# Alternating expert places, a blocked gather, a down product on four column quarters and a sum into x on four row tiles

## The chip, the cores and the metric

The kernel runs on one core of one Trainium2 chip. The metric is device time in microseconds (us). The kernel before takes 1996.44 us, the median of three runs (1993.87 to 1998.35).

The names of the profile: PE is TensorE, PEld its weight loads, DVE VectorE, ACT ScalarE, POOL GpSimd. SP is the engine that issues all transfers here (SPq is its queue). L1545 is line 1545 of the kernel before.

## The reference

Two layers on 256 latent tokens and 256 context tokens of width 1024, all in float32. The even layer has attention beside a convolution and then a dense feed-forward block; the odd layer has a state-space mixer and then the expert block. This is the part that the change touches:

```python
def moe_swiglu(h, w_router, w1, w3, w2):
    ...
    logits = (hf @ w_router).astype(jnp.float32)
    top_v, top_i = lax.top_k(logits, TOP_K)
    top_w = jax.nn.softmax(top_v, axis=-1)
    gates = jnp.sum(jax.nn.one_hot(top_i, N_EXPERTS, dtype=jnp.float32) * top_w[..., None], axis=1)
    out = jnp.zeros_like(hf)
    for e in range(N_EXPERTS):
        out = out + gates[:, e:e + 1].astype(hf.dtype) * swiglu(hf, w1[e], w3[e], w2[e])
```

with `swiglu = (silu(h @ w1) * (h @ w3)) @ w2`, 8 experts, 2 for each token, a hidden width of 3584. Only the 256 latent tokens go through it. The weights of the eight experts are 8 x 3 x 1024 x 3584 x 4 bytes = 352 MB. After the sum into x comes a last RMSNorm.

## The kernel before

The kernel computes the two layers one after the other; the change leaves all work up to the router as it is. In the expert stage each expert's tokens are gathered into slots of 32, called groups. There are eight **places**, worked off in order. Place 0 is always expert 0; the other seven experts are ranked by their token counts (`places`, L1579) and put in places 1 to 7 from the fullest on. The number of groups of each place is fixed in the program (`G`, L1429): 3, 3, 3, 3, 2, 2, 2, 2. Behind the last place two further passes over all places stand under a condition, for tokens that did not fit (`moe`, L1643).

The work of a place is a list of units (`expert`, L1471). `gather` (L1432) selects the tokens by a product with a 0/1 matrix `pm` and scales them, result `xe`. `up` multiplies by w1, then w3: first the hidden rows 0 to 2047, then 2048 to 3583. The weights are the moving operand and 32 tokens of `xe` the stationary one, so that four column tiles of TensorE work beside one another, each on another part of the weights (L1491: 512 columns each in the first part, 384 in the second). `turn` transposes the hidden activations to `hT` (L1514). `down` (L1545) multiplies them by w2, 512 columns at a time: two halves of the 1024 outputs, and for each half two partial sums on the four column tiles, result `y`, one PSUM bank for each group. `scatter` multiplies `y` by the layer's gate row `g2` (L1555), and brings it back to token order by a product with the transposed map `PT` (L1562; two row tiles of 64, which also add the two partial sums), and DVE adds it with the gate of the router into x (L1566). `PT` comes from transposes of `pm` on TensorE (L1466) with a copy by ACT.

Each place reads 46 weight **transfers** (`load`, L131): 16 of 1 MiB for the first part of w1 and w3 (8 KB in a row per partition), 16 of 768 KB for the second part (6 KB rows), 14 of 1 MiB for w2 (two rows of 4 KB). They go through a **ring** of 16 buffers of 1 MiB, in the fixed order of use; `run` (L150) issues up to `AHEAD` = 14 transfers ahead of the unit that it writes out. A transfer waits on SP until the matmuls that read its buffer last are done. All transfers are issued by SP in one order; the expert's number for places 1 to 7 is read into SP's registers first (L1606). PSUM has five banks under the name `h` and three under `y` (L1779).

The gather of the next place and the map's transposes are spread between the units (`later`); the scatter of a place comes two units into the next place. A scheduler then settles each engine's order; the instructions of an engine run in that order.

Of the kernel before, what the change touches and what calls it, by code (L numbers as in the profile page):

```python
# [19 lines left out]
P = 128  # L20
D = 1024
# [6 lines left out]
NCONST = 1032  # L28


def host_consts():

    kc = np.zeros((P, NCONST), np.float32)
# [18 lines left out]
    for j in range(4):  # L52
        kc[32 * j:32 * j + 8, C_SEL8:C_SEL8 + 8] = np.eye(8)
    return kc


class Pair:
# [4 lines left out]
    def __call__(self, k, s=slice(0, 512)):  # L62
        return tuple(t[k // 4][:, k % 4, s] for t in self.t)

# [11 lines left out]
class Net:  # L76
# [44 lines left out]
    def load(self, view, pool=None):  # L121

        pieces = view if isinstance(view, list) else [(slice(0, P), view)]
# [161 lines left out]
    def columns2(self):  # L285
        A, cols, row = self.A, self.cols_fn, self.row_fn
        kc = self.ecp.tile([P, NCONST - C_LE], F32, name="kc")
        self.nc.sync.dma_start(kc, A["kc"][:, C_LE:])
# [1084 lines left out]
    def route(self):  # L1373
# [4 lines left out]
        self.h2 = mp.tile([P, 2, D], F32, name="h2")  # L1378
        m8 = rt.tile([P, 2, 8], F32, name="m8")
# [41 lines left out]
        self.g2 = mp.tile([P, 512], F32, name="g2r")  # L1421
        g2 = self.g2row.rearrange("k p -> (k p)")
        for i in range(2):
            nc.sync.dma_start(self.g2[64 * i:64 * i + 64], g2[512 * i:512 * i + 512].partition_broadcast(64))
# [4 lines left out]
    G = [3, 3, 3, 3, 2, 2, 2, 2]  # L1429
    SS = ((0, 512), (2048, 384))  # L1430

    def gather(self, e, pos, n_g):  # L1432
# [4 lines left out]
        Pm = self.wk([P, 2, 3, 4, 32], "pm", bufs=2)[:, :, :n_g]  # L1437
        x = self.wk([P, KD, 96], "xe", bufs=2)[:, :, :n]
        PT = self.wk([P, 3, 256], "PT", bufs=2)

        def work():
            slots = self.iota[:, :n].rearrange("p (g t) -> p g t", g=n_g).unsqueeze(2).to_broadcast([P, n_g, 4, 32])
            for b in range(2):
                nc.vector.tensor_scalar(Pm[:, b], slots, pos[:, b, e:e + 1], None, op0=ALU.is_equal)
            yield
            for q in range(2):
                pt = self.ps("h")
                for i in range(4):
                    k = 4 * q + i
                    for b in range(2):  # L1450
                        nc.tensor.matmul(pt[:, i * n:(i + 1) * n].rearrange("p (g t) -> p g t", g=n_g),  # L1451
                                         self.h2[:, b, k * P:(k + 1) * P], Pm[:, b, :, 0], start=b == 0, stop=b == 1)
# [7 lines left out]
                yield  # L1460

        def turn():
            for g in range(n_g):
                pt = self.ps("h")
                for b in range(2):
                    nc.tensor.transpose(pt[:, b * P:(b + 1) * P], Pm[:, b, g].rearrange("p r t -> p (r t)"), self.ident)  # L1466
                nc.scalar.copy(PT[:, g], pt[:, 0:256])
# [332 lines left out]
```

## Time and profile before

| | |
|---|---|
| median of 3 runs | 1996.44 us (1993.87 to 1998.35) |
| profiled execution | 1998.1 us |
| its span, first to last instruction | 1996.3 us, granted TensorE clock 0.975 of 2.4 GHz |
| PE busy | 1860.1 us (93%) |
| DVE, ACT, POOL busy | 734.5, 519.0, 257.7 us |
| HBM read | 485.14 MB, 244 GB/s over the span |
| expert stage, place 0 to the end | 1088.7 to 1996.3 us |

How to read the profile: a busy share says how long an engine had an instruction in it, not that it did its best. The chain of waits starts at the last instruction and goes back, at each step to what released it; an engine or a transfer that stands on it in a stretch sets the time of that stretch. In the view by time, the idle time before a row and its releaser stand in brackets. Matmuls in float32 take two passes, so the profile counts two instructions where the program has one.

### The profile page before, as it was taken

Reading aid. Unit: us, or ns where it says so; the run is one execution under the profiler, and the core shown is the slowest. Engines: PE = TensorE matmul, PEld = TensorE weight load, DVE = VectorE, ACT = ScalarE, POOL = GpSimd, SP = SyncE. Lnnn points to the kernel's source line nnn. Section 1 sums busy time; section 2 is a strip of 40 time slices with the busy share of each in tenths; the row PEclk is TensorE's granted clock in tenths of the full one; section 3 lists DMA queues with packets and bytes.
Section 4 is the critical chain, followed back from the end, with each engine's and each line's share of the span. In section 5 each row is a group of like instructions: output and inputs, shape, how many; then the busy total and the mean of one; then the engine's idle time right before and its main releaser. Section 6 shows DMA issues by size and latency. Waiting matters only on the chain.

```text
span 1996.3 us, 29959 instructions
## 1 busy us (share of the span) xinstructions
PE 1860.1 (93%) x12586; PEld 1057.2 (53%) x12586; DVE 734.5 (37%) x1079; ACT 519.0 (26%) x948; POOL 257.7 (13%) x239
## 2 busy tenths in 40 slices
PE   6999999999999989899898999999999999979795
PEld 3685366888888868666566343433434343313121
DVE  3496545333343458988975000101001011101011
ACT  3434443222223247466653000000000000000000
POOL 0154000000000024476650000000000000000000
PEclk8999989999999999999898999999999999999998
DMA  8544575323322332221338999898998999999996
GB/s 295 179 136 155 202 201 179 127 85 106 106 85 95 117 118 85 84 64 64 116 127 313 306 418 364 336 403 289 416 344 342 415 389 416 413 417 413 418 413 236
DMA packets 136429, 488.31 MB, mean 245 GB/s; under 512 B 10432, under 2 KB 15192, under 8 KB 119896
## 3 DMA queue, kind: packets, MB, share of 16 engines
q1 hardware_dynamic: 136280, 486.25, 65.0%
q8 instruction: 103, 1.69, 0.4%
q14 instruction: 46, 0.38, 0.1%
HBM read 485.14 MB, written 1.07 MB: 244 GB/s over the span
## 4 chain that ended last, share of the span: by engine, by line
PE 69%; DMA 14%; DVE 10%; ACT 2%; issue 2%; POOL 1%; SPq 0%; DVEq 0%; ACTq 0%; POOLq 0%
PE h L1491 20%; PE g L226 9%; PE g L227 9%; PE g L228 9%; DMA t<-in_od_ex_w_dram 9%; PE y L1545 8%; DVE cv L1055 5%; DMA raw<-in_od_ex_w_dram 4%; PE h L1562 2%; PE g L330 1%; PE h L1451 1%; PE o L758 1%; PE g L735 1%; DVE whl L147 1%; DMA raw<-in_ev_w_in_dram 1%
## 5 line engine op out<-in xcount | busy, mean ns | idle before, releaser
L1491 PE MATMUL h<-t,xe 128*32 128x384 f32 (+1 forms) x2880 | 288.4, 541 | 13.5 <-DMA t<-in_od_ex_w_dram 13.3
L227 PE MATMUL g<-t,whl 128*128 128x512 f32 (+1 forms) x608 | 237.7, 391 | 0.0
L228 PE MATMUL g<-t,whl 128*128 128x512 f32 (+1 forms) x608 | 236.1, 394 | 0.7 <-POOL whl L147 0.7
L226 PE MATMUL g<-t,whl 128*128 128x512 f32 (+1 forms) x608 | 233.3, 395 | 1.4 <-ACT opad L1033 0.7
L1491 PE MATMUL h<-raw,xe 128*32 128x512 f32 (+1 forms) x2240 | 223.3, 540 | 8.1 <-DMA raw<-in_od_ex_w_dram 8.1
L147 DVE TENSOR_TENSOR whl<-raw,whl 128x1024 fp32r<-128x1024 f32 x109 | 138.6, 1274 | 201.0 <-ACT whl L144 200.6
L144 ACT CAST whl<-raw 128x1024 fp32r<-128x1024 f32 x129 | 134.7, 1050 | 265.6 <-PE g L228 231.2
L1491 PEld LDWEIGHTS h<-t,xe 128*32 128x32 f32 x2880 | 92.0, 110 | 195.3 <-issue 167.9
L1502 DVE TENSOR_TENSOR g<-g,h 128x512 f32<-128x512 f32 (+1 forms) x40 | 24.8, 621 | 458.3 <-PE h L1491 365.4
L411 POOL TENSOR_SCALAR rsv<-sst 128x1 f32<-128x1 f32 (+1 forms) x15 | 5.5, 364 | 1353.6 <-DVE sst L404 1353.5
L227 PE MATMUL g<-whl,t 128*128 128x512 f32 (+1 forms) x432 | 169.3, 394 | 6.4 <-DVE whl L147 3.2
L228 PE MATMUL g<-whl,t 128*128 128x512 f32 (+1 forms) x432 | 166.8, 394 | 0.0
L226 PE MATMUL g<-whl,t 128*128 128x512 f32 (+1 forms) x432 | 162.4, 395 | 2.9 <-DVE t L624 1.4
L1491 PEld LDWEIGHTS h<-raw,xe 128*32 128x32 f32 x2240 | 73.7, 110 | 150.9 <-issue 134.7
L1545 PE MATMUL y<-t,hT 128*32 128x512 f32 x1288 | 144.9, 594 | 8.7 <-DMA t<-in_od_ex_w_dram 8.6
L226 PEld LDWEIGHTS g<-t,whl 128*128 128x128 f32 x608 | 116.0, 192 | 30.1 <-issue 2.3
L228 PEld LDWEIGHTS g<-t,whl 128*128 128x128 f32 x608 | 116.0, 191 | 25.3 <-issue 1.9
L227 PEld LDWEIGHTS g<-t,whl 128*128 128x128 f32 x608 | 116.4, 191 | 23.4 <-issue 0.9
L1519 ACT COPY hT<-h 128x512 f32<-128x512 f32 (+1 forms) x24 | 12.8, 533 | 418.1 <-PE h L1514 417.8
L1545 PE MATMUL y<-raw,hT 128*32 128x512 f32 x952 | 107.9, 594 | 8.8 <-DMA raw<-in_od_ex_w_dram 8.8
L1545 PEld LDWEIGHTS y<-t,hT 128*32 128x32 f32 x1288 | 43.0, 110 | 103.0 <-issue 77.8
L227 PEld LDWEIGHTS g<-whl,t 128*128 128x128 f32 x432 | 82.5, 191 | 27.0 <-DVE whl L147 4.7
(348 smaller groups left out, 2189.3 us busy)
## 6 DMA issues: line engine op xcount, KB each, us to landing
t<-in_od_ex_w_dram SPq DMA_DIRECT2D x135, 1024.0 KB, 12.9
raw<-in_od_ex_w_dram SPq DMA_DIRECT2D x105, 1024.0 KB, 13.9
t<-in_od_ex_w_dram SPq DMA_DIRECT2D x72, 768.0 KB, 9.3
raw<-in_od_ex_w_dram SPq DMA_DIRECT2D x56, 768.0 KB, 10.8
raw<-in_ev_ff_w_dram SPq DMA_DIRECT2D x32, 1024.0 KB, 5.2
raw<-in_ev_ada_w_dram SPq DMA_DIRECT2D x24, 1024.0 KB, 6.9
raw<-in_od_ada_w_dram SPq DMA_DIRECT2D x24, 1024.0 KB, 5.3
raw<-in_od_w_in_dram SPq DMA_DIRECT2D x20, 1024.0 KB, 5.2
```

The lines of the kernel that those rows point to most:

```text
L144: self.nc.scalar.copy(hv, v[:, k0:k0 + m])
L147: eng.tensor_tensor(lv, v[:, k0:k0 + m], hv.bitcast(F32), op=ALU.subtract)
L226: mm(out, l[0], r[0], start=start, stop=False)
L227: mm(out, l[0], r[1], start=False, stop=False)
L228: mm(out, l[1], r[0], start=False, stop=stop)
L330: nc.tensor.matmul(st["p"][32 * j:32 * j + 32], self.cs[:, k, 6 - 2 * i:38 - 2 * i], wv, start=k < 4, stop=k >= 4, tile_position=(0, 32 * j))
L735: nc.tensor.matmul(sc[c][:, :nk], self.qT[s, r, b * P:(b + 1) * P], self.kT[s, :nk], start=True, stop=True, tile_position=(64 * c, 0))
L1055: nc.vector.scalar_tensor_tensor(v, pads[i + j][:, 0:ns, t:t + 256], self.cvw(t, c0 + i + j), v, op0=ALU.mult, op1=ALU.add)
L1491: nc.tensor.matmul(st[i][g][32 * p:32 * p + 32, :n], st["x"][:, k, 32 * g:32 * g + 32], wv[:, n * p:n * p + n], start=k == 0, stop=k == KD ...
L1502: nc.vector.tensor_mul(st["g"][g], st["g"][g], st[1][g][:, :n])
L1545: nc.tensor.matmul(st["y"][g][r:r + 32], st["hT", s][:, c, g, 32 * p:32 * p + 32], w[:, 512 * half:512 * half + 512], start=s == 0 and k == 1,
L1562: nc.tensor.matmul(pt[half], st["PT"][r, g, b * P:(b + 1) * P], ys[r, g], start=g == 0, stop=g == n_g - 1, tile_position=(64 * half, 0))
```

## The change

Only the expert stage changes.

- The places have 3, 2, 3, 2, 3, 2, 3, 1 groups, and the ranks are put in them in the order 3, 0, 4, 1, 5, 2, 6 (0 is the fullest of the seven).
- `gather` builds `pm` once, without the four copies, and runs as one unit between the second `up` and the second `turn` of the place before.
- `PT` is no longer transposed on TensorE. The positions of all tokens are transposed once, written to DRAM (`posd`), and for each place read back by a transfer that spreads its row to all partitions (`prow`, 128 KB in 512-byte runs); DVE compares it with the slot numbers.
- `down` works on four quarters of 256 columns, one for each column tile; each column tile holds the whole sum of its quarter, two groups share a bank. `y` is multiplied by `g2` right behind it. Twelve of a place's 14 w2 transfers now take pairs of consecutive rows, 8 KB in one piece; the hidden activations are transposed in the matching order.
- The sum into x takes four row tiles of 32, each with its quarter of 256 columns, in four banks of `h`; DVE adds eight pieces of 256 columns. It is one unit behind the first `up` of the next place.
- The ring has 17 buffers, 16 transfers go ahead, PSUM has six banks `h` and two `y`. The expert's number is read when a place's first transfer is written out.

```diff
+C_SLOT, C_RANK, C_CAP = NCONST, NCONST + 3, NCONST + 10
...
+GROUPS = (3, 2, 3, 2, 3, 2, 3, 1)
+RANKS = (3, 0, 4, 1, 5, 2, 6)
...
+    kc[:, C_SLOT:C_SLOT + 3] = i[:, None] % 32 + 32 * np.arange(3)
+    kc[:, C_RANK:C_RANK + 7] = RANKS
+    kc[:, C_CAP:C_CAP + 8] = 32 * np.array(GROUPS)
...
-        self.g2 = mp.tile([P, 512], F32, name="g2r")
+        self.g2 = mp.tile([P, 256], F32, name="g2r")
...
-    G = [3, 3, 3, 3, 2, 2, 2, 2]
     SS = ((0, 512), (2048, 384))
 
-    def gather(self, e, pos, n_g):
+    def gather(self, e, n_g):
...
-        Pm = self.wk([P, 2, 3, 4, 32], "pm", bufs=2)[:, :, :n_g]
+        Pm = self.wk([P, 2, 96], "pm", bufs=2)[:, :, :n]
         x = self.wk([P, KD, 96], "xe", bufs=2)[:, :, :n]
...
-        def turn():
-            for g in range(n_g):
-                pt = self.ps("h")
-                for b in range(2):
-                    nc.tensor.transpose(pt[:, b * P:(b + 1) * P], Pm[:, b, g].rearrange("p r t -> p (r t)"), self.ident)
-                nc.scalar.copy(PT[:, g], pt[:, 0:256])
-                yield
-        return x, PT, work(), turn()
...
+    def slot_map(self, e, n_g):
+
+        nc = self.nc
+        r = self.wk([P, 256], "prow", bufs=2)
+        nc.sync.dma_start(r.rearrange("p (b t) -> p b t", b=2), self.posd[:, e].partition_broadcast(P))
+        PT = self.wk([P, 3, 256], "PT", bufs=2)
+        for g in range(n_g):
+            nc.vector.tensor_scalar(PT[:, g], r, self.slot[:, g:g + 1], None, op0=ALU.is_equal)
+        return PT
+
+    def pos_rows(self, pos):
+
+        nc = self.nc
+        self.pos = pos
+        pt = self.ps()
+        nc.tensor.transpose(pt[:16, 0:P], pos.rearrange("p b e -> p (b e)"), self.ident)
+        r = self.wk([16, P], "posr", bufs=1)
+        nc.scalar.copy(r, pt[:16, 0:P])
+        d = self.drp.tile([16, P], F32, name=self.nm("posd"))
+        nc.sync.dma_start(d, r)
+        self.posd = d.rearrange("(b e) p -> b e p", b=2)
...
         def down(s):
-            nch = self.SS[s][1] // P
+            r0, n = 4 * self.SS[s][0] // 4, self.SS[s][1]
+            rows = lambda r, m: (lambda w: w[:, r:r + m])
+            pair = lambda w: w.rearrange("o (i j) n -> i (o j) n", j=2)
+
+            pieces = []
+            for p in range(4):
+                for c in range(n // 256):
+                    f = rows(r0 + n * p + 256 * c, 256)
+                    pieces.append((lambda w, f=f: pair(f(w)), [(p, 2 * c), (p, 2 * c + 1)]))
+            if n % 256:
+                for p in (0, 2):
+                    f = rows(r0 + n * p, 2 * n)
+                    pieces.append((lambda w, f=f: f(w).rearrange("o (s i) n -> i (o s) n", s=2)[n - P:n],
+                                   [(p, n // P - 1), (p + 1, n // P - 1)]))
 
             def begin():
                 if s == 0:
-                    st["y"] = [self.ps("y") for _ in range(n_g)]
+                    st["y"] = [self.ps("y") for _ in range(0, n_g, 2)]
 
             def mm(k, wv, _):
-
-                p, c = divmod(k, nch)
-                st["w", k % 2] = wv, p, c
-                if k % 2 == 0:
-                    return
+                p, c = pieces[k // 2][1][k % 2]
                 for g in range(n_g):
-                    for half in range(2):
-                        for j in range(2):
-                            w, p, c = st["w", j]
-                            r = 64 * half + 32 * j
-                            nc.tensor.matmul(st["y"][g][r:r + 32], st["hT", s][:, c, g, 32 * p:32 * p + 32],
-                                             w[:, 512 * half:512 * half + 512], start=s == 0 and k == 1,
-                                             stop=s == 1 and k == 4 * nch - 1, tile_position=(0, r))
-
-            k0 = 16 * s
-            return Unit([w2[:, k0 + r:k0 + r + 2] for r in range(0, 4 * nch, 2)], mm, begin, None, False)
+                    for q in range(4):
+                        nc.tensor.matmul(st["y"][g // 2][32 * q:32 * q + 32, g % 2 * 256:g % 2 * 256 + 256],
+                                         st["hT", s][:, c, g, 32 * p:32 * p + 32], wv[:, 256 * q:256 * q + 256],
...
+                                         tile_position=(0, 32 * q))
+
+            return Unit([self.weights("od_ex_w2", e, [P, 2, D], f) for f, _ in pieces], mm, begin,
+                        evict if s else None, False)
+
+        def evict():
+            st["PT"] = self.slot_map(e, n_g)
+            st["ys"] = ys = self.wk([P, 4, 256], "ys", bufs=1)
+            for g in range(0, n_g, 2):
+                m = min(2, n_g - g)
+                nc.vector.tensor_tensor(ys[:, g:g + m], st["y"][g // 2][:, :256 * m].rearrange("p (g n) -> p g n", g=m),
+                                        self.g2.unsqueeze(1).to_broadcast([P, m, 256]), op=ALU.mult)
 
         def scatter():
...
+            pt = [self.ps("h") for _ in range(4)]
             for b in range(2):
...
                 for g in range(n_g):
...
+                    for q in range(4):
+                        r = slice(32 * q, 32 * q + 32)
+                        nc.tensor.matmul(pt[q][:, b * 256:b * 256 + 256], st["PT"][r, g, b * P:(b + 1) * P],
+                                         st["ys"][r, g], start=g == 0, stop=g == n_g - 1, tile_position=(32 * q, 0))
+            for q in range(4):
+                for b in range(2):
+                    x = self.X[2 + b][:, 256 * q:256 * q + 256]
+                    nc.vector.scalar_tensor_tensor(x, pt[q][:, b * 256:b * 256 + 256], self.gate[:, b, e:e + 1], x,
+                                                   op0=ALU.mult, op1=ALU.add)
...
+        return ([Unit(begin=take), up(0, 0, "od_ex_w1"), up(0, 1, "od_ex_w3")],
+                [turn(0), up(1, 0, "od_ex_w1"), up(1, 1, "od_ex_w3")], [turn(1), down(0), down(1)],
+                Unit(begin=scatter))
...
+            if e and e not in self.at:
+                self.at[e] = self.nc.values_load(self.ati[0:1, e - 1:e], engines=[mybir.EngineType.SP], min_val=1,
+                                                 max_val=7)
...
-        nc.vector.tensor_tensor(one, sq(rank, 1), sq(self.iota[:, 0:7], 2), op=ALU.is_equal)
+        nc.vector.tensor_tensor(one, sq(rank, 1), sq(self.rank_at, 2), op=ALU.is_equal)
...
+            a, b, c, d = self.expert(e, n_g[e])
+            units += a + scatter + b + gather(e + 1) + c
+            if e == 0 and now:
+                units.insert(2, Unit(begin=now))
+            scatter = [d]
+        return units + scatter
...
-    AHEAD = 14
+    AHEAD = 16
...
-            with psum("psm", h=5, y=3) as net.psp, tc.tile_pool(name="mp", bufs=1) as net.mp:
+            with psum("psm", h=6, y=2) as net.psp, tc.tile_pool(name="mp", bufs=1) as net.mp:
...
-                    net.rings = ["t8"] * 9 + [net.rawp] * 3 + [net.hlp] * 3 + [rawm]
+                with tc.tile_pool(name="ep", bufs=1) as net.wp, tc.tile_pool(name="rawm", bufs=2) as rawm:
+                    net.rings = ["t8"] * 9 + [net.rawp] * 3 + [net.hlp] * 3 + [rawm] * 2
```

TensorE's order in place 0, where the second `up` ends and the down product begins. `xe` are the gathered tokens, `raw` and `t8` weight buffers, `hT` the transposed activations, `y` the results. Before:

```order
L1491 MATMUL h_1456_8315<-raw_1441_8199,xe_1374_7738 32x384 x4
L1545 MATMUL y_1465_8431<-t8_1442_8213,hT_1432_8159 32x512 x4
L1545 MATMUL y_1466_8432<-t8_1442_8213,hT_1432_8159 32x512 x4
L1545 MATMUL y_1467_8433<-t8_1442_8213,hT_1432_8159 32x512 x4
L1545 MATMUL y_1465_8431<-t8_1444_8231,hT_1432_8159 32x512 x4
```

And now:

```order
L1515 MATMUL h_1457_8237<-raw_1435_8076,xe_1374_7742 32x384 x4
L1468 MATMUL h_1467_8365<-pm_1465_8361,h2_7691 128x64 x8
L1468 MATMUL h_1468_8378<-pm_1465_8361,h2_7691 128x64 x8
L1548 MATMUL h_1470_8392<-ka_92,g_1451_8227 128x128 x3
L1548 MATMUL h_1471_8397<-ka_92,g_1452_8228 128x128 x3
L1548 MATMUL h_1472_8402<-ka_92,g_1453_8229 128x128 x3
L1580 MATMUL y_1474_8409<-raw_1440_8112,hT_1436_8093 32x256 x8
L1580 MATMUL y_1475_8410<-raw_1440_8112,hT_1436_8093 32x256 x4
L1580 MATMUL y_1474_8409<-raw_1444_8129,hT_1436_8093 32x256 x8
L1580 MATMUL y_1475_8410<-raw_1444_8129,hT_1436_8093 32x256 x4
```

The next place's gather and the second transposes now stand ahead of the down product, and a w2 buffer is read by 24 matmuls of 256 columns (12 for each of its two rows) where 12 of 512 read it.

SP's order at the first w2 transfers of the second place worked (place 1). Before:

```order
L131 DMA raw_1529_8978<-in_od_ex_w3_dram 128x1536
L131 ISA
L131 DMA raw_1530_8992<-in_od_ex_w2_dram 128x2x1024
L131 ISA
L131 DMA raw_1532_9010<-in_od_ex_w2_dram 128x2x1024
L131 ISA
```

And now, with `prow` the position row of place 4:

```order
L148 DMA raw_1513_8940<-in_od_ex_w3_dram 128x1536
L148 ISA
L148 DMA raw_1521_9001<-in_od_ex_w2_dram 128x2048
L1483 DMA prow_1811_12085<-posd_1424_7973 128x2x128
L148 ISA
L148 DMA raw_1524_9013<-in_od_ex_w2_dram 128x2048
```

A position row stands between two weight transfers; the rows of places 5, 6 and 7 stand in the same way one place further on each, and the first four stand in place 0's second part.

## Rows read from the trace of the kernel before

**Rows 1.** the page's 40 slices of 49.9 us: TensorE's busy tenths, GB/s moved

```profile
PE   6999999999999989899898999999999999979795
...
GB/s 295 179 136 155 202 201 179 127 85 106 106 85 95 117 118 85 84 64 64 116 127 313 306 418 364 336 403 289 416 344 342 415 389 416 413 417 413 418 413 236
```

**Rows 2.** chain of waits, expert stage: start us, us, engine, tile, line

```profile
1088.66 41.34 PE h L1491 x384
1130.00 1.53 PE h L1514 x12
...
1143.35 21.45 PE h L1491 x264
...
1313.53 41.34 PE h L1491 x384
...
1377.29 3.74 PE h L1562 x12
...
1433.45 3.55 PE h L1451 x32
1436.99 41.34 PE h L1491 x384
...
1668.05 20.27 DMA t<-in_od_ex_w_dram
```

**Rows 3.** TensorE in order of time, last places: start us, busy us, [idle before]

```profile
1748.01 1.92 PE L1491 MATMUL h<-raw,xe 128*32 128x512 f32 x16 [0.65 <-DMA raw<-in_od_ex_w_dram]
...
1785.24 1.92 PE L1491 MATMUL h<-raw,xe 128*32 128x512 f32 x16 [0.59 <-DMA raw<-in_od_ex_w_dram]
...
1800.55 1.92 PE L1545 MATMUL y<-t,hT 128*32 128x512 f32 x16 [0.61 <-DMA t<-in_od_ex_w_dram]
...
1907.85 1.92 PE L1545 MATMUL y<-t,hT 128*32 128x512 f32 x16 [0.54 <-DMA t<-in_od_ex_w_dram]
...
1943.31 1.92 PE L1545 MATMUL y<-t,hT 128*32 128x512 f32 x16 [0.48 <-DMA t<-in_od_ex_w_dram]
...
1971.44 1.92 PE L1545 MATMUL y<-raw,hT 128*32 128x512 f32 x16 [0.61 <-DMA raw<-in_od_ex_w_dram]
```

**Rows 4.** chain of waits, the end after the last landing

```profile
1973.98 1.92 PE y L1545 x16
1975.91 2.85 PE h L1562 x12
```

**Rows 5.** SP's transfer issues in order of time, around the stage's start

```profile
1077.13 0.33 SPq L131 DMA_DIRECT2D raw<-in_od_ex_w_dram  x1
1091.44 20.93 SPq L131 DMA_DIRECT2D t<-in_od_ex_w_dram  x9
```

**Rows 6.** TensorE in order of time, 32-column weights and 256 columns

```profile
1073.98 0.64 PE L1310 MATMUL t<-BT,cs 128*32 128x256 f32 x8 [0.52 <-ACT BT L1302]
1074.47 0.64 PE L1310 MATMUL t<-CT,cs 128*32 128x256 f32 x8
```

**Rows 7.** weight loads in order of time, four of one round

```profile
1974.44 0.13 PEld L1545 LDWEIGHTS y<-raw,hT 128*32 128x32 f32 x4 [0.30 <-issue]
```

**Rows 8.** the page's transfer issues: count, KB each, us from issue to landing

```profile
t<-in_od_ex_w_dram SPq DMA_DIRECT2D x135, 1024.0 KB, 12.9
...
raw<-in_ev_ff_w_dram SPq DMA_DIRECT2D x32, 1024.0 KB, 5.2
```

**Rows 9.** groups by line and form, expert stage: busy us, mean ns, idle before

```profile
L1566 DVE SCALAR_TENSOR_TENSOR x<-h,gate,x 128x512 f32<-128x512 f32 x32 | 23.0, 748 | 54.4 <-PE h L1562 54.4
...
L1502 DVE TENSOR_TENSOR g<-g,h 128x512 f32<-128x512 f32 x20 | 13.7, 687 | 309.0 <-PE h L1491 309.0
...
L1502 DVE TENSOR_TENSOR g<-g,h 128x384 f32<-128x384 f32 x20 | 11.1, 554 | 149.4 <-issue 91.8 <-PE h L1491 56.4
```

**Rows 10.** windows: length, busy by engine (PE first), granted clock, DMA share, GB/s

```profile
20.00:30.00 10.00, 4.56 (x19) 2.37 (x20) 3.80 (x12) 2.57 (x4) 0.00 (x0) 0.50 0.83 312
...
1740.00:1780.00 40.00, 31.08 (x260) 7.40 (x256) 0.00 (x0) 1.20 (x2) 0.00 (x0) 1.00 1.02 420
```

More of the change, by code (lines that the diff above doesn't have):

```diff
@@ L63, in __call__, with __init__ @@
         return tuple(t[k // 4][:, k % 4, s] for t in self.t)
+class View:
+    def __init__(self, shape, get):
+        self.shape, self.get = shape, get
 class Unit:
@@ L121, in load @@
     def load(self, view, pool=None):
+        if isinstance(view, View):
+            view = view.get()
         pieces = view if isinstance(view, list) else [(slice(0, P), view)]
@@ L1502, in end, with take @@
                         nc.vector.tensor_mul(st["g"][g], st["g"][g], st[1][g][:, :n])
-            return Unit([w[:, k:k + 1, c0:c0 + 4 * n] for k in range(KD)], mm, begin, end, False)
+            view = lambda k: self.weights(name, e, [P, 1, 4 * n], lambda w: w[:, k * P:(k + 1) * P, c0:c0 + 4 * n]
+                                          .rearrange("o p n -> p o n"))
+            return Unit([view(k) for k in range(KD)], mm, begin, end, False)
+        def take():
+            st["x"] = self.xe
         def turn(s):
-            nch = self.SS[s][1] // P
+            n = self.SS[s][1]
             def call():
@@ new lines, in scatter @@
+            for q in range(4):
+                for b in range(2):
+                    x = self.X[2 + b][:, 256 * q:256 * q + 256]
[4 more added lines that the diff above has]
+                Unit(begin=scatter))
@@ L1579, in places, with weights, get @@
+    def weights(self, name, e, shape, f):
+        def get():
+            if e and e not in self.at:
+                self.at[e] = self.nc.values_load(self.ati[0:1, e - 1:e], engines=[mybir.EngineType.SP], min_val=1,
+                                                 max_val=7)
+            return f(self.A[name][0][bass.ds(self.at[e], 1) if e else slice(0, 1)])
+        return View(shape, get)
     def places(self):
@@ L1613, in places @@
                 place(dst[:, b, 1:8], src[:, b, 1:8])
[L1614 to L1617 removed]
+        self.gate = gate
+        self.pos2 = pos
         nc.vector.tensor_copy(over[:, 0:1], cnt[:, 0:1])
         place(over[:, 1:8], cnt[:, 1:8])
[L1620 removed]
+        nc.vector.tensor_sub(over, over, self.cap)
         mx = small("mxc", 1)
@@ L1624, in places, with experts, gather, call @@
         nc.vector.tensor_copy(self.cnt, mx)
-        self.cap = cap
-    def experts(self, gather, n_g):
-        units, last = [], []
-        for e in range(8):
-            nxt = (lambda e=e: gather(e + 1)) if e < 7 else None
-            a, b, c = self.expert(e, n_g[e], nxt)
-            units += a + last + b
-            last = c
-        return units + last
+    def experts(self, n_g, now=None):
+        units, scatter = [], []
+        def gather(e):
+            def call():
+                self.xe, work = self.gather(e, n_g[e])
+                work()
+            return [Unit(begin=call)] if e < 8 else []
+        for e in range(8):
+            a, b, c, d = self.expert(e, n_g[e])
[4 more added lines that the diff above has]
+        return units + scatter
     def ring(self):
```

104 lines of the change are left out of this document (34 added, 70 removed).

## The prediction

> **What bounds the kernel now.** I read the page's slices first: through the expert stage (from about 1050 us) TensorE stands at 9 tenths while the transfers run at 289 to 418 GB/s [rows 1]. Both look full, so the next view is the chain of waits. It shows one stage with two limits. From 1088.66 us, where place 0 begins, it is TensorE alone; from 1668.05 us it is a chain of weight transfers to the last landing [rows 2]. The change of limit follows the sizes. The first four places have three groups of 32 tokens; one takes 1436.99 - 1313.53 = 123.46 us, and what TensorE reads is there before it asks. The last four have two groups and are through sooner than their weights come: each transfer starts a burst, then TensorE waits [rows 3].
>
> From those waits a transfer can be priced. 1 MiB in 8 KB rows (first part of w1, w3): (1785.24 - 1748.01) / 15 = 2.48 us. 1 MiB of w2, in 4 KB rows: (1971.44 - 1943.31) / 11 = 2.56 us. One whole place, 46 transfers, from last burst to last burst: 1907.85 - 1800.55 = 107.30 us [rows 3]. What remains for the 16 transfers of 768 KB is (107.30 - 16 x 2.48 - 14 x 2.56) / 16 = 1.99 us. Eight places cannot go below 8 x 107.3 = 858 us of transfers, whatever TensorE does. Before spends 1973.98 - 1091 = 883 us between the first buffer that comes free and the last landing [rows 4, 5], with 16 transfers already in: the four slow places let the queue idle, and this cannot be bought back behind them.
>
> **The change part by part.**
>
> *Order of places.* Sizes go from 3,3,3,3,2,2,2,2 to 3,2,3,2,3,2,3,1: 19 groups for 20. By the reference's router the tokens are 81 for expert 0 and 91, 90, 83, 60, 52, 39, 16 for the others by rank. By the new ranks the places hold 81, 60, 91, 52, 90, 39, 83, 16 in 96, 64, 96, 64, 96, 64, 96, 32 slots, so no further pass is entered.
>
> *Down product.* Per group 112 matmuls of 512 columns become 224 of 256 (as the profile counts, two passes each). Four column tiles run side by side: 41.34 / 384 = 107.7 ns per matmul of 512 columns, 21.45 / 264 = 81.3 ns per one of 384 [rows 2]. The line through both gives 54.8 at 256, so a group stays at 12.3 us. No long stream of 256 columns is in the trace. Below: 53.8, half of 107.7. Above: eight such matmuls with 32-column weights begin 74.47 - 73.98 = 0.49 us before the next eight, 61 ns each [rows 6]. I take 54.8, because weight loads seem to be no limit: four of 32 columns overlap and are over in 0.13 us [rows 7], and the streams of four take 0.22.
>
> *TensorE per place.* Three groups: 41.34 (first part of w1 and w3), 1.53 (transposes) [rows 2], 384 x 81.3 = 31.2 (second part), 3.55 (next gather) [rows 2], 1.1 (the second transposes, 9 for 12), 3 x 12.3 = 36.9: 115.6 us. Added is the sum into x of the place before. Of a three-group one's 24 matmuls 12 now take 3.74 us [rows 2]; afterwards it has 48 matmuls of 256 columns on four row tiles: 2.6 us if they stream as above, 5.3 at the gather's 3.55 / 32 = 111 ns with 128-column weights. I take the upper. The transposes of the token map (before L1466) go. The sum now holds four of six h banks, and DVE's eight sums release them: 3 us of waiting allowed. So a three-group place is 122 us and a two-group place 27.6 + 20.8 + 24.6 + 5 + 5.3 + 3 = 86 us; a pair 208 us, against 2 x 106.8 for the transfers.
>
> *Transfers per place.* 12 of 14 w2 transfers get 8 KB rows: 12 x 0.08 = 1 us less, 106.3 (107.3 if rows were not the reason). New is the position row, 128 KB per place in 512-byte runs: by bytes 0.3 us, at most a 1 MiB transfer's 2.48; I take 0.5.
>
> *Place 0.* The ring (17 buffers for 16) is full when TensorE starts at 1088.66; before, too, SP issued nothing between 1077.13 and 1091.44 [rows 5]. While the first part is multiplied, a buffer comes free every 2.58 us and is filled in 1.99, so the queue idles. From the second part on buffers come free every 1.95 us and take 2.48: transfers fall behind at 1088.66 + 41.34 + 1.53 + 1.95 = 1133.5 us and run without a break. Tile 63, the last that place 0 releases, would be issued by 1206, and TensorE releases it at 1088.66 + 115.6 + 1 = 1205: just in balance.
>
> *After that.* The ring holds 39 us of transfers. A two-group place takes about 20 off, a three-group one gives 15 back: never full again, so the queue never stops. Place 7, one group, needs about 50 us of TensorE beside 106 us of transfers.
>
> *SP.* Each position row stands among weight loads. From the fifth on its buffer waits for DVE's map of the place two back, queued behind the sums: about 5.3 + 3.9 + 1 = 10 us in which SP issues no weights. A weight load lands 12.9 us after issue when the queue is full [rows 8], so that cover is just enough. Only in place 1, where SP is 17 tiles ahead, could some be lost: 0 to 5 us, I take 1.
>
> *Sum.* First landing after 1133.5: a lone 1 MiB load lands 5.2 us after issue [rows 8], 2.7 above its share. Then 11 x 2.48 + 2 x 2.56 = 32.4 for the rest of place 0, 7 x 106.3 = 744.1, four position rows 2, SP 1: 1133.5 + 2.7 + 32.4 + 744.1 + 3 = 1915.7 us. The tail is now 1996.3 - 1973.98 = 22.3 us [rows 4]. In it 1.92 of down and 2.85 of sum [rows 4] shrink by some 2 us with one group; DVE's four sums of 512 columns at 748 ns become eight of 256, at about 748 - 2 x 133 = 482 ns by the slope of 687 to 554 for 128 columns [rows 9], 0.9 us more; I leave it at 22.3. The span is 1938, and 1.8 around it (1998.1 - 1996.3) makes 1940 us. The profiled run stood 1.7 above the median of its three, so I predict 1938.
>
> *The clock in place 7.* With one group a burst is 8 x 107.7 = 0.86 us out of 2.48. At 31.08 busy of 40 us the granted clock was 1.00 (2.4 GHz), at 4.56 of 10 it was 0.50 (1.2 GHz) [rows 10]. At half clock place 7 needs about 100 us, still under 106; the last burst and sum take 2 us more. The Trainium skill (TensorE: Matmul & The Clock Gate, Part 1) says that half rate is the default and activity lifts it; the trace agrees with its two levels, and by that rule the sum would be 1940.
>
> **Rivals.**
>
> *Small matmuls cost somewhat more (chance 0.10).* At 61 ns the ring absorbs it: about 1941. At 65 a group is 2.3 us dearer, place 0 ends at 1212 and each of three pairs takes 208 + 11.5 = 219.5; then 15 x 1.99 + 34.8 = 65 us of place 7's transfers remain: 1212 + 658.5 + 65 + 2.7 + 22.4 = 1961. For it: the 0.49 us; against: they are two bursts that wait on ScalarE copies.
>
> *Slower: weight loads stop hiding (0.06).* The place is the down product. If the four loads of a round (0.13 us [rows 7]) stand in front of their four streams, a matmul costs (0.22 + 0.13) / 4 = 87 ns and a group 7.2 us more. Place 0 ends at 1227, a pair takes 244: 1227 + 732 + 67 + 22.4 = 2048 us. It decides from about 73 ns on, where the time is that of before. Against it: with 512 columns the same four loads add nothing, 107.7 ns where 0.43 + 0.13 us for four would be 140. The Trainium skill (TensorE: Matmul & The Clock Gate, Part 3, The mechanism) speaks for it: loads overlap running matmuls only when the row group differs, and the four column tiles share all rows. By that rule the 512-column rows would show 140 ns too; the trace does not bear it out, hence the small chance.
>
> *SP's waits empty the queue (0.08).* If cover is gone behind the last four position rows, each costs 10 us: 1978. For it: 12.9 us against 10 is thin; against: in the stage's second half SP runs only as far ahead as the queue lets it, so the sum it waits for is then done.
>
> *The slots do not suffice (0.01).* A further pass reads all weights again, at least 8 x 107 us: near 2800. Against: the counts above.
>
> *Something else (0.05), half of it without gain or slower.*
>
> **How the numbers follow.** The forecast has 0.70: 1926 (no gap in place 0, the smaller bounds) to 1952 (w2 unchanged, +7; SP +5; dear position rows). The range for 8 in 10 goes up to 1962, to take in the dearer matmul. What a measurement tells from no change is 0.2%, 4 us. Faster: 0.70 + 0.10 + 0.08 + 0.02 = 0.90; same 0.03; slower 0.07.
>
> **What would show it.** Right: the chain from about 1134 us on transfers, no TensorE stretch above some tens of us; GB/s at 41x in every slice to the last; transfers 2.48 us apart in w2; a mean round of down near 0.22 us; last landing near 1916. Wrong: TensorE on the chain in the down line after place 0, rounds of 0.3 us or more; SP waiting long on the position rows with the transfers' share falling; a second pass over the weights.

## The result and the profile after

The changed kernel takes 1943.28 us (median of 4 runs, 1942.08 to 1947.99) against 1995.15 (1993.19 to 1998.35): a ratio of 0.9743, 95% interval 0.9721 to 0.9764. 1938 was forecast, with 1926 to 1962 as the range. The profiled run took 1943.61 us, with a span of 1941.8.

The page of the changed kernel in 40 slices of 48.5 us: TensorE's busy tenths, its granted clock, GB/s.

```profile
PE   6999998999999989988888899999998999899964
...
PEclk8999989999999999999999899999999999999975
...
GB/s 290 170 162 137 235 188 182 130 87 109 87 87 109 87 122 109 87 64 89 65 162 195 304 386 418 412 418 416 418 417 418 417 416 409 418 418 413 418 412 205
```

The slices of the expert stage that went from 289 to 418 GB/s [rows 1] now stand at 409 to 418 from the 25th to the last but one. TensorE still shows 8 and 9 tenths. The chain of waits in the expert stage (start us, us, engine, tile, line):

```profile
1086.71 20.74 PE h L1515 x192
...
1165.97 36.40 PE y L1580 x672
1202.37 27.47 PE h L1515 x256
1229.84 2.80 PE h L1604 x48
1232.64 1.16 PE h L1548 x8
...
1283.36 41.20 PE h L1515 x384
1324.56 2.46 PE h L1604 x31
...
1364.60 36.40 PE y L1580 x672
1401.00 4.91 PE h L1515 x45
1405.91 19.79 DMA t<-in_od_ex_w_dram
...
1495.37 41.41 PE h L1515 x384
...
1562.16 17.40 DMA t<-in_od_ex_w_dram
...
1722.25 28.53 PE h L1515 x264
...
1791.62 37.20 PE y L1580 x672
1828.82 19.77 DMA raw<-in_od_ex_w_dram
...
1898.72 19.86 DMA raw<-in_od_ex_w_dram
...
1918.62 1.98 PE y L1580 x16
...
1921.10 2.13 PE h L1604 x16
```

L1515 is `up`, L1580 the down product, L1604 the sum into x. TensorE leads for three places (place 3 begins at 1401.00), then mostly transfers do, 262 us earlier than before [rows 2]; twice more TensorE leads, for 67 us from 1495.37 and for 107 us from 1722.25. The chain goes back from a transfer's issue to the matmuls that freed its buffer, and of the 15 to 20 us from issue to landing it does not tell how many are waiting in the queue. So it can name TensorE also where the queue is full; that the queue does not stop is read from the GB/s.

I measure the stage from place 0's first matmul to the last place's first matmul of the sum: before 1975.91 - 1088.66 = 887.3 us [rows 2, 4], after 1921.10 - 1086.71 = 834.4. Of the 54.5 us by which the spans differ, 52.9 lie there, 2.0 in an earlier start of place 0, and what follows the sum is 0.3 longer. In the profiled runs below place 0 starts anywhere from 1082 to 1090 us, which is most of the spread of the times. The stage repeats within 1 to 2 us (834.4, 834.4 and 835.4 in three profiles of the changed kernel, 839.8 and 841.4 in two of before_alternating below) and so tells more than a time does.

The transfers one by one: TensorE in order of time in place 3 (start us, us, shape, count, [idle before]).

```profile
1443.24 1.50 PE L1515 MATMUL h<-raw,xe 128*32 128x384 f32 x16 [0.33 <-DMA raw<-in_od_ex_w_dram]
...
1456.31 1.50 PE L1515 MATMUL h<-raw,xe 128*32 128x384 f32 x16 [0.34 <-DMA raw<-in_od_ex_w_dram]
...
1469.99 1.93 PE L1580 MATMUL y<-t,hT 128*32 128x256 f32 x32 [0.69 <-DMA t<-in_od_ex_w_dram]
...
1477.45 1.93 PE L1580 MATMUL y<-t,hT 128*32 128x256 f32 x32 [0.56 <-DMA t<-in_od_ex_w_dram]
...
1490.24 1.93 PE L1580 MATMUL y<-raw,hT 128*32 128x256 f32 x32 [0.60 <-DMA raw<-in_od_ex_w_dram]
1492.79 1.93 PE L1580 MATMUL y<-raw,hT 128*32 128x256 f32 x32 [0.62 <-DMA raw<-in_od_ex_w_dram]
```

w2 in 8 KB rows comes every (1477.45 - 1469.99) / 3 = 2.49 us, the two pieces in 4 KB rows 2.55 apart (2.56 in [rows 3]), 768 KB every 13.07 / 7 = 1.87. From place 3's last burst to the last landing it is (1918.62 - 1492.79) / 4 = 106.5 us a place.

Landing takes longer than before, 12.9 us then [rows 8]. A row of the page's transfer issues of the changed kernel (count, KB, us from issue to landing):

```profile
t<-in_od_ex_w_dram SPq DMA_DIRECT2D x130, 1024.0 KB, 19.5
```

### The profile page after: what moved, and what is told of

Same layout as the page of the kernel before. It is cut to its first block, busy times and chain, and to the rows that moved or that the text cites. A ratio compares the mean times of both kernels' runs of the same rounds, so it can differ in the third digit from the quotient of the medians.

```text
span 1941.8 us, 33657 instructions
## 1 busy us (share of the span) xinstructions
PE 1796.3 (93%) x14444; PEld 1120.8 (58%) x14444; DVE 728.4 (38%) x1118; ACT 509.5 (26%) x927; POOL 259.1 (13%) x231
## 4 chain that ended last, share of the span: by engine, by line
PE 64%; DMA 19%; DVE 11%; ACT 3%; issue 2%; POOL 1%; SPq 0%; DVEq 0%; ACTq 0%; POOLq 0%
PE h L1515 17%; PE g L243 9%; PE g L244 9%; DMA t<-in_od_ex_w_dram 9%; PE g L245 9%; DMA raw<-in_od_ex_w_dram 8%; PE y L1580 7%; DVE cv L1072 6%; PE g L347 1%; PE h L1468 1%; PE o L775 1%; PE g L752 1%; DVE whl L164 1%; DMA raw<-in_ev_w_in_dram 1%; PE h L1604 1%
## 5 line engine op out<-in xcount | busy, mean ns | idle before, releaser
L1515 PE MATMUL h<-t,xe 128*32 128x512 f32 (+1 forms) x2576 | 252.7, 542 | 12.8 <-DMA t<-in_od_ex_w_dram 12.7
L1515 PE MATMUL h<-raw,xe 128*32 128x384 f32 (+1 forms) x2288 | 230.2, 551 | 13.6 <-DMA raw<-in_od_ex_w_dram 13.6
L1515 PEld LDWEIGHTS h<-t,xe 128*32 128x32 f32 x2576 | 92.2, 110 | 164.6 <-issue 109.0
L1515 PEld LDWEIGHTS h<-raw,xe 128*32 128x32 f32 x2288 | 82.4, 111 | 153.1 <-issue 95.8
L1580 PE MATMUL y<-t,hT 128*32 128x256 f32 x2336 | 136.9, 391 | 13.1 <-DMA t<-in_od_ex_w_dram 13.1
L1523 ACT ACTIVATE g<-h 128x512 f32<-128x512 f32 (+1 forms) x38 | 20.7, 544 | 451.0 <-PE h L1515 451.0
L1580 PE MATMUL y<-raw,hT 128*32 128x256 f32 x1920 | 111.1, 387 | 8.9 <-DMA raw<-in_od_ex_w_dram 8.9
L1580 PEld LDWEIGHTS y<-t,hT 128*32 128x32 f32 x2336 | 74.4, 112 | 73.8 <-DMA t<-in_od_ex_w_dram 21.1
L1594 DVE TENSOR_TENSOR ys<-y,g2r 128x512 f32<-128x512 f32 (+1 forms) x12 | 6.6, 577 | 262.5 <-PE y L1580 262.5
## 6 DMA issues: line engine op xcount, KB each, us to landing
t<-in_od_ex_w_dram SPq DMA_DIRECT2D x130, 1024.0 KB, 19.5
```

The costliest lines, as they stand in the source:

```text
L1515: nc.tensor.matmul(st[i][g][32 * p:32 * p + 32, :n], st["x"][:, k, 32 * g:32 * g + 32], wv[:, n * p:n * p + n], start=k == 0, stop=k == KD ...
L1523: nc.scalar.activation(st["g"][g], st[0][g][:, :n], AF.Silu)
L1580: nc.tensor.matmul(st["y"][g // 2][32 * q:32 * q + 32, g % 2 * 256:g % 2 * 256 + 256], st["hT", s][:, c, g, 32 * p:32 * p + 32], wv[:, 256 ...
```

## The experiments

Theory 1 was the prediction's: the stage is bound by transfers, and the gain is that they no longer stop. The rivals put the gain into TensorE's cheaper products, or into the order of the places alone. Each kernel was timed beside the kernel before on the same chip.

**The changed kernel again** (after_again, no edit). 

> The changed kernel as it is, for comparison with the others of this call. Both theories: 1943 us, and the last weight landing at about 1918.6 us of the span.

Measured 1941.78 us (1940.86 to 1946.49), ratio 0.9729 (0.9707 to 0.9750).

**A group more in the last place** (last_two).

```diff
-GROUPS = (3, 2, 3, 2, 3, 2, 3, 1)
+GROUPS = (3, 2, 3, 2, 3, 2, 3, 2)
```

> The last place gets two groups instead of one, so 20 groups as in the kernel before. Theory 1 (the transfers set the time from about 1130 us on): the last landing stays at 1918.6 us within 1 us, the tail is dearer by one group (some 1 to 2 us less the clock, which should stay at 1.00): 1943 us, within 2 us. Theory 2 (TensorE's work sets the time, and the saved group is part of the gain): one more group is 28 x 4 x 2 matmuls of 54 ns and two parts of 13.8 and 10.4 us, together 36 us: up to 1979 us.

Measured 1942.88 us (1940.93 to 1945.25), stage 836.1. The group that the change saves is worth at most the 1.7 us by which the stage is longer, little more than two profiles of one kernel differ by, and not the 36 of theory 2: TensorE's work in place 7 is covered by the transfers.

**w2 in 4 KB rows again** (w2_short_rows).

```diff
-            pair = lambda w: w.rearrange("o (i j) n -> i (o j) n", j=2)
+            pair = lambda w: w.rearrange("o (j i) n -> i (o j) n", j=2)
```

(and the transposes in the old order of columns).

> Twelve of the 14 w2 transfers of a place again bring two rows of 4 KB to a partition instead of one of 8 KB (the hidden activations are transposed in the plain order to match). Theory 1: w2 transfers 2.56 us apart instead of 2.48, 0.96 us per place, 7.7 places in the stretch that the transfers set: +7 us, 1950 us. Rival (the spacing differs for another reason, the place in memory or what TensorE reads at that time): 1943 us.

Measured 1949.64 us, spread from 1943.38 to 1956.35, so the time alone says little; the stage says 840.1, 5.7 more. TensorE in order of time in this kernel's down product shows the spacing of the kernel before, 2.55 us:

```profile
1467.02 1.93 PE L1580 MATMUL y<-t,hT 128*32 128x256 f32 x32 [0.41 <-DMA t<-in_od_ex_w_dram]
1469.58 1.93 PE L1580 MATMUL y<-t,hT 128*32 128x256 f32 x32 [0.63 <-DMA t<-in_od_ex_w_dram]
```

**Position rows issued by POOL** (pool_rows). SP's waits behind them were my first suspect for the landing that came later than forecast.

```diff
-        nc.sync.dma_start(r.rearrange("p (b t) -> p b t", b=2), self.posd[:, e].partition_broadcast(P))
+        nc.gpsimd.dma_start(r.rearrange("p (b t) -> p b t", b=2), self.posd[:, e].partition_broadcast(P))
...
-        nc.sync.dma_start(d, r)
+        nc.gpsimd.dma_start(d, r)
```

> The position rows and their source are issued by POOL's queue instead of SP's. Theory 1 with the missed term (SP's waits on the position rows in place 0 held back weight loads that the queue never made up): no drop of the transfers at 1110 to 1130 us, the last landing 3 to 5 us sooner, 1939 us. Rival (the ring is full there anyway, the loads are made up before 1130 us, and the 3 us by which the landing came later than forecast are spread over the places): 1943 us within 1 us; slower by up to 3 us if POOL's issue costs the queue something.

Measured 1945.58 us (1944.29 to 1947.48), stage 834.6: no gain, so this suspicion falls. Windows of place 0 (busy by engine, PE first; clock, DMA share, GB/s), first of after_again, then of this kernel:

```profile
1100.00:1110.00 10.00, 10.00 (x97) 2.85 (x90) 0.00 (x0) 1.93 (x4) 0.00 (x0) 1.00 0.90 291
1110.00:1120.00 10.00, 10.00 (x100) 3.03 (x96) 1.40 (x5) 0.00 (x0) 0.00 (x0) 1.00 0.66 212
1120.00:1130.00 10.00, 10.00 (x104) 4.21 (x100) 2.75 (x4) 1.17 (x2) 0.00 (x0) 1.00 1.02 418
1130.00:1140.00 10.00, 10.00 (x132) 4.03 (x128) 0.00 (x0) 0.00 (x0) 0.00 (x0) 1.00 0.94 362
```

```profile
1100.00:1110.00 10.00, 10.00 (x97) 2.95 (x93) 0.00 (x0) 1.93 (x4) 0.75 (x1) 1.00 0.94 315
1110.00:1120.00 10.00, 10.00 (x96) 2.99 (x92) 1.40 (x5) 0.00 (x0) 2.31 (x4) 1.00 0.96 295
1120.00:1130.00 10.00, 10.00 (x96) 4.06 (x92) 2.76 (x4) 1.17 (x2) 0.62 (x1) 1.00 0.90 323
1130.00:1140.00 10.00, 10.00 (x130) 4.03 (x124) 0.00 (x0) 0.00 (x0) 0.00 (x0) 1.00 0.93 349
```

The hole of 212 GB/s closes, but the 40 us move 12.8 MB in both: the loads that wait behind the rows are made up at once.

**The old order with the new products** (old_order).

```diff
-GROUPS = (3, 2, 3, 2, 3, 2, 3, 1)
-RANKS = (3, 0, 4, 1, 5, 2, 6)
+GROUPS = (3, 3, 3, 3, 2, 2, 2, 1)
+RANKS = (0, 1, 2, 3, 4, 5, 6)
```

> The changed kernel with the places back in their old order: four places of three groups first, then three of two and the one of one (3,3,3,3,2,2,2,1); the blocked gather, the quarters of the down product, the row tiles of the sum and the 8 KB rows of w2 stay. Theory 1 (transfers carry the gain, and they run unbroken only if a two-group place follows each three-group one): TensorE carries the first four places at the changed kernel's 118 us each, so place 3 ends near 1086.7 + 115.7 + 3 x 118 = 1556; the queue is then full and some 384 us of transfers are left, so the last lands near 1943, and with a tail of 23 us and 2 us around the span the time is about 1968 us (1960 to 1976), some 25 us above the changed kernel. Rival (the gain is TensorE's cheaper products, whatever the order): within 3 us of the changed kernel. Rival (the whole gain is the order): 1995 us.

Measured 1975.61 us (1972.19 to 1977.03), ratio 0.9884 (0.9863 to 0.9904), stage 868.5: nearest to theory 1, some 8 us over it. Windows of this kernel:

```profile
1400.00:1500.00 100.00, 100.00 (x1321) 49.48 (x1323) 9.82 (x23) 5.51 (x11) 0.00 (x0) 1.00 0.95 367
1500.00:1600.00 100.00, 100.00 (x1369) 52.07 (x1365) 10.68 (x25) 5.76 (x13) 0.00 (x0) 1.00 1.02 417
```

While three-group places follow one another TensorE is never idle and the queue moves 367 GB/s; place 4 begins at 1558.56, 2.5 us later than expected. The other 5 us come after it: the last landing is 393 us on, 33 less than four places of 106.5, where I had put the ring's head start at 42. Against the kernel before, the new products and rows alone thus bring 887.3 - 868.5 = 18.8 us.

**The new order with the old products** (before_alternating). The kernel before with

```diff
-    G = [3, 3, 3, 3, 2, 2, 2, 2]
+    G = [3, 2, 3, 2, 3, 2, 3, 2]
+    RANKS = (3, 0, 4, 1, 5, 2, 6)
```

(and the ranks compared with that list).

> The kernel before with its places alternating (3,2,3,2,3,2,3,2, the ranks placed to fit); its down product, its sum into x, its gather and its 4 KB rows of w2 stay. Theory 1 (the order alone makes the transfers run unbroken): after the first part of place 0 the transfers set the pace at about 107.3 us a place, so the time is 1945 to 1955 us, at most 10 us above the changed kernel; and a place of three groups (about 139 us of TensorE, from before's first places) with one of two would have to fit into 2 x 107.3 = 214.6 us. If that pair does not fit, TensorE sets the pace again and the excess comes four times. Rival (without the quarters and the row tiles the order gives nothing): about 1995 us.

Measured 1948.66 us (1946.24 to 1949.44), ratio 0.9751 (0.9731 to 0.9770), stage 839.8. The order alone brings 47.5 of the 52.9 us (45.9 by a second profile, below). But theory 1 in its plain form is not what the trace shows. A window of this kernel:

```profile
1200.00:1900.00 700.00, 698.90 (x6557) 257.92 (x6550) 74.36 (x127) 45.06 (x94) 0.00 (x0) 1.00 1.02 414
```

TensorE is busy in 698.9 of 700 us while the queue moves 414 GB/s. Rows of its chain of waits, the first two one pair of places apart:

```profile
1586.31 20.60 PE y L1546 x192
...
1799.46 20.60 PE y L1546 x192
...
1885.54 15.40 DMA t<-in_od_ex_w_dram
```

A pair takes TensorE 213.15 us with the old products (the expectation's 139 us for a place of three groups is a slip, [rows 2] give 123.46). The transfers want 2 x 106.5 = 213.0 with the new rows, and 2 x 107.3 = 214.6 with this kernel's own by [rows 3]; here they are what ends last, from 1885.54 us. The two limits are level, by chance.

**A smaller ring** (small_ring).

```diff
-    AHEAD = 16
+    AHEAD = 8
...
-                    net.rings = ["t8"] * 9 + [net.rawp] * 3 + [net.hlp] * 3 + [rawm] * 2
+                    net.rings = ["t8"] * 9
```

> The changed kernel with 9 ring places of 1 MiB instead of 17 mixed ones, and loads asked for 8 units ahead instead of 16. Theory 1 (in a three-group place TensorE falls some 12 us behind the transfers and in a two-group place it gains some 25 us; a lead of 9 tiles, 9 x 2.48 = 22 us, is nearly enough for that): the transfers stay the bound after place 0, and the time is within 6 us of the changed kernel. Rival (the depth of the ring carries the gain, since the transfers of a three-group place need all of its slots): above 1958 us.

Measured 1958.88 us (1957.11 to 1964.01), stage 852.0: 17.6 us more, as the rival's bound had it. Its reason, that the places need the slots, is not borne out: from 1200 to 1900 us the queue moves 410 to 417 GB/s in each 100 us. The loss lies before place 0. Windows there, first of after_again, then of this kernel:

```profile
1040.00:1060.00 20.00, 19.00 (x96) 15.81 (x96) 10.71 (x13) 7.33 (x9) 0.90 (x2) 1.00 0.68 251
1060.00:1080.00 20.00, 13.70 (x79) 10.84 (x78) 10.04 (x41) 7.16 (x15) 0.90 (x2) 0.83 1.02 409
```

```profile
1040.00:1060.00 20.00, 19.01 (x92) 15.71 (x91) 9.67 (x11) 7.33 (x9) 0.90 (x2) 1.00 0.58 211
1060.00:1080.00 20.00, 14.22 (x77) 11.58 (x76) 12.34 (x58) 7.26 (x15) 0.90 (x2) 0.72 0.31 113
```

40 GB/s less over 20 us and 296 less over the next 20 are 6.7 MB that are not there when the stage begins, 16 us at 418 GB/s. So the ring's size counts as a head start.

**Order and rows, old products** (order_rows): before_alternating with w2 in pairs of rows as in the changed kernel,

```diff
+                    pieces.append((w[:, r:r + 256].rearrange("o (i j) n -> i (o j) n", j=2),
+                                   [(p, 2 * c), (p, 2 * c + 1)]))
...
-            return Unit([w2[:, k0 + r:k0 + r + 2] for r in range(0, 4 * nch, 2)], mm, begin, None, False)
+            return Unit([f for f, _ in pieces], mm, begin, None, False)
```

> The kernel before with its places alternating and, beside that, w2 in rows of 8 KB (the two rows of a pair next to each other in memory, the transposes that feed the down product taking every second column); the down product on halves of 512 columns, the sum into x on two row tiles, the gather and the transposed places of the kernel before stay. In the alternating kernel without the rows TensorE was busy in every stretch from 1200 to 1900 us (99.6 of 100 us and more) at 213.15 us for a pair of places, and the transfers of a pair with 8 KB rows want 2 x 106.5 = 213.0 us. Theory A (TensorE's dear products and the transfers are level, so the shorter transfers find TensorE in the way): 0 to 2 us below the alternating kernel, some 1947 to 1949 us, and the cheap products are what lets the changed kernel take the rows' gain. Theory B (the order and the rows are the whole change, the cheap products are worth nothing): 1941 to 1944 us, level with the changed kernel.

Measured 1948.24 us (1945.96 to 1948.45), stage 839.8, the same as without the rows. Timed beside it:

**The alternating kernel again** (alternating_again). 

> The kernel before with its places alternating and nothing else, once more, as the base of order_rows: 1946 to 1950 us. If the order alone carries nearly the whole gain, it lies 5 to 8 us above the changed kernel.

1948.04 us (1946.25 to 1953.00), stage 841.4.

**The changed kernel a third time** (after_third). 

> The changed kernel unaltered, the base of this call: 1941 to 1945 us.

1943.26 us (1941.18 to 1947.91), stage 835.4. Theory A's numbers come out: the rows alone give nothing. The end of order_rows, TensorE in order of time:

```profile
1901.63 12.22 PE L1563 MATMUL y<-t,hT 128*32 128x512 f32 x112
1913.67 12.20 PE L1563 MATMUL y<-raw,hT 128*32 128x512 f32 x112
1925.82 3.70 PE L1579 MATMUL h<-ys,PT 64*128 64x512 f32 x16
```

The whole last down product runs without a stop: the weights are there, and TensorE is what ends last. Cheap products without the rows (840.1) and rows without the cheap products (839.8) stand where the order alone stands (839.8, 841.4); only the whole change gives the 5 us more. That the rows are worth something only beside the rest of the change is thus shown: 5.7 us there, nothing with the old products. That it is the cheaper products which let them pay is argued from TensorE never being idle; it is not shown apart. The changed kernel also has one ring buffer more than these two kernels, which may be worth 2.5 us by the next run (ring_plus1), and one group less in its last place: with two groups there it stands at 836.1 (last_two), 3.7 below order_rows. No run has the changed kernel with 16 buffers. By the times the step is about 5 us too, 1943.26 against 1948.24, though two of the five runs of the changed kernel reach into the other's range.

**An eighteenth place in the ring** (ring_plus1).

```diff
-    AHEAD = 16
+    AHEAD = 17
...
-    with tc.tile_pool(name="ep", bufs=1) as net.wp, tc.tile_pool(name="rawm", bufs=2) as rawm:
-                    net.rings = ["t8"] * 9 + [net.rawp] * 3 + [net.hlp] * 3 + [rawm] * 2
+    with tc.tile_pool(name="ep", bufs=1) as net.wp, tc.tile_pool(name="rawm", bufs=3) as rawm:
+                    net.rings = ["t8"] * 9 + [net.rawp] * 3 + [net.hlp] * 3 + [rawm] * 3
```

> The changed kernel with an eighteenth ring place of 1 MiB and loads asked for 17 units ahead. Theory (what the ring holds when place 0 begins is a head start, and each place of it is worth its transfer's time; the small ring, 8 places fewer, moved 40 and 296 GB/s less over two stretches of 20 us before place 0, 6.7 MB or 16 us at 418 GB/s, and took 16 us more): 2 to 2.5 us below the changed kernel of the same call, about 1939 to 1941 us. Rival (17 places are enough, the queue is unbroken with them): level with the changed kernel, within 1 us.

Measured 1938.88 us (1936.66 to 1940.47), ratio 0.9710 (0.9690 to 0.9730), stage 831.9: 2.5 us less than the changed kernel's 834.4, the price of one 1 MiB transfer. All five runs lie below all 14 of the changed kernel (1940.86 to 1947.99). It is faster than both kernels.

The stage of every run, from place 0's first matmul to the last place's first matmul of the sum (us; time is the median):

| run | time | place 0 begins | last sum begins | stage |
|---|---|---|---|---|
| the kernel before | 1995.15 | 1088.66 | 1975.91 | 887.3 |
| the changed kernel | 1943.28 | 1086.71 | 1921.10 | 834.4 |
| after_again | 1941.78 | 1084.04 | 1918.47 | 834.4 |
| after_third | 1943.26 | 1089.62 | 1925.02 | 835.4 |
| last_two | 1942.88 | 1083.84 | 1919.92 | 836.1 |
| w2_short_rows | 1949.64 | 1081.96 | 1922.08 | 840.1 |
| pool_rows | 1945.58 | 1085.86 | 1920.47 | 834.6 |
| old_order | 1975.61 | 1085.74 | 1954.28 | 868.5 |
| before_alternating | 1948.66 | 1087.12 | 1926.90 | 839.8 |
| alternating_again | 1948.04 | 1089.09 | 1930.53 | 841.4 |
| order_rows | 1948.24 | 1086.05 | 1925.87 | 839.8 |
| small_ring | 1958.88 | 1082.62 | 1934.65 | 852.0 |
| ring_plus1 | 1938.88 | 1084.25 | 1916.11 | 831.9 |

## Why the prediction was right, by its own steps

The mechanism held: a queue that runs from place 0's second part to the last landing, at the price per place that was read off the kernel before. w2_short_rows shows that transfers set the time: dearer transfers with the same work on TensorE make the stage 5.7 us longer. The signs and the sizes:

- *The signs.* One that was to show it right did not come: the chain goes over to transfers at 1405.91 us and not at about 1134, and TensorE comes back for 67 and 107 us. One half of a sign of being wrong did come, the down product's line on the chain after place 0 (1364.60, 1791.62), though its rounds of four take 0.22 us and not 0.3. The GB/s, the spacing of w2's transfers (2.49 us) and the last landing (1918.62) came as forecast, and these decide. The forecast named as a sign a view in which a full queue cannot be told from a waiting one.
- *Down product.* 36.40 / 672 = 54.2 ns per matmul, where 54.8 was taken between 53.8 and 61. The rivals of dearer small matmuls (61 and more) and of unhidden weight loads (87 ns) are out. The rule of the Trainium skill (TensorE: Matmul & The Clock Gate, Part 3, The mechanism) that loads overlap only when the row group differs does not fit this trace: four column tiles share all rows here, and at 256 columns their loads add nothing that shows, 54.2 ns being half of the 107.7 at 512. (The same section names loads into a background weight buffer beside that rule; no run here tells whether these are such.)
- *Sum into x.* Mis-sized: 2.80 us for 48 matmuls, 58 ns each, near the lower bound of 2.6 and not the 5.3 taken (a two-group place's 32 take 2.46 us, 77 ns each); and of the 3 us of waiting for h banks nothing shows, the transposes follow at 1232.64 without a gap.
- *TensorE per place.* So the places were some 5 us cheaper than forecast: 1401.00 - 1283.36 = 117.6 us for 122, 1283.36 - 1202.37 = 81.0 for 86. It changed nothing, since the pair's 208 was already below the transfers.
- *Transfers per place.* 106.5 us, position row included, against 106.3 + 0.5. The 768 KB price was too high, 1.87 for 1.99: worked out as a remainder, it had taken in some 1.9 us a place that belong to something else; for the sum of a place this makes no difference.
- *Place 0.* Here the time was missed. From place 0's start to the last landing 827.0 us were forecast; it took 831.9. After place 3's last burst it was 1.4 us quicker than forecast, so 6.3 went before it. A window of the changed kernel:

```profile
1090.00:1130.00 40.00, 40.00 (x369) 12.86 (x361) 3.89 (x9) 2.51 (x5) 0.00 (x0) 1.00 0.86 288
```

  One 768 KB transfer for every buffer that comes free, each 2.58 us, would be 305 GB/s; 288 is 0.7 MB or 1.6 us less. pool_rows shows that SP's position rows are not the reason. The rest, 4.7 us, stays open. The trace has one candidate that the sum left out: the queue thins before the last landing. The last 8.62 us before it:

```profile
1910.00:1918.62 8.62, 5.35 (x56) 1.60 (x48) 0.00 (x0) 0.00 (x0) 0.00 (x0) 0.70 0.51 204
```

  At 418 GB/s they would have carried 1.8 MB more, 4.4 us of transfers. The sum priced every transfer at the full rate and allowed 2.7 us for the first landing only. This fits the loss ahead of place 3's last burst, since parts of later loads have moved by the time that a load has landed: from that burst to the last landing the queue moved 411 GB/s x 425.8 us = 175.0 MB, 1.2 less than four places hold (44.04 each). No run tests how much of the 4.7 us this explains.
- *SP's waits later.* In place 1 one position row waits 6.4 us for DVE's map of place 0, and the queue falls from 417 to 390 GB/s for 10 us, 0.6 us of transfers; 1 was taken. The rival of an emptied queue (10 us a place) is out. Transfers wait longer in the queue, 19.5 us and not 12.9, so the cover was larger than the forecast's.
- *The tail.* 1941.8 - 1918.62 = 23.2 us after the last landing for 22.3. The clock in place 7 did fall, as the prediction had left open. Windows of the changed kernel, and TensorE in order of time at its end:

```profile
1800.00:1900.00 100.00, 76.77 (x943) 28.32 (x935) 5.49 (x12) 2.15 (x4) 0.00 (x0) 0.88 1.01 415
1900.00:1920.00 20.00, 14.25 (x132) 4.67 (x128) 0.00 (x0) 0.00 (x0) 0.00 (x0) 0.59 0.73 298
```

```profile
1913.57 1.07 PE L1580 MATMUL y<-t,hT 128*32 128x256 f32 x16 [0.68 <-DMA t<-in_od_ex_w_dram]
1916.09 1.93 PE L1580 MATMUL y<-raw,hT 128*32 128x256 f32 x16 [1.45 <-DMA raw<-in_od_ex_w_dram]
```

```profile
1913.57:1914.64 1.07, 1.07 (x16) 0.42 (x16) 0.00 (x0) 0.00 (x0) 0.00 (x0) 1.00 0.47 191
1916.09:1918.02 1.93, 1.93 (x16) 0.59 (x16) 0.00 (x0) 0.00 (x0) 0.00 (x0) 0.50 0.51 206
```

  The same 16 matmuls take 1.07 us at a granted clock of 1.00 (the 2.4 GHz level) and 1.93 at 0.50 (1.2); the burst still fits between two landings. With two groups in the last place (last_two), where the granted clock was 1.00 from 1800 to 1920 us, the tail was 1940.6 - 1917.17 = 23.4 us, so the lower clock cost no more than the saved group gave.

What the prediction did not do is price the parts apart. It added the cheaper products and the order in one sum; had it worked out the old products in the new order (213 us a pair, as before_alternating measured, against 214.6 for the transfers by its own price), it would have seen that the order alone nearly frees the queue and that the other edits can add only some 5 us. The new order alone measured 1948.66, inside the stated range too, so that the forecast came true says little for the prices of the products.

## What to carry to other kernels

Where two engines or an engine and a queue take turns as the limit, first sum each one's work over the whole stage: if the sums are level and only the order makes them wait, mixing long and short pieces can gain more than cheaper pieces do: here 47.5 us against 18.8. Two limits that are level hide each other, so an edit to one can be worth nothing until the other is cut as well (here the 8 KB rows); price the edits one by one and together. In a stage bound by transfers a buffer is worth its own transfer's time once, as a head start, if there is idle queue time ahead of the stage to fill it.

## What the runs showed of the hardware

- TensorE with four row tiles of 32, 128-column weights and 256 columns in float32 took 58 ns per counted matmul in runs of 48 (2.80 us) and 77 in runs of 32 (2.46 us); four column tiles with 32-column weights took 54.2.
- Rows of 8 KB in DRAM came at 2.49 us per MiB, rows of 4 KB at 2.55, both with the queue full; it moved 409 to 418 GB/s in every slice of 48.5 us for some 730 us.
- The granted clock fell in a place where bursts of 16 matmuls stood about 2.5 us apart: 0.88 of full speed over the stretch of 100 us in which that place begins, 0.59 over the next 20.
